# A decoder layer in full precision on one Trainium2 core: each weight split once, the pair of parts kept in DRAM

## The chip, the core and the metric

The kernel runs on one core of one Trainium2 chip. A core has five engines that run side by side and wait for one another by semaphores: TensorE (PE in the profile; its weight loads are PEld), VectorE (DVE), ScalarE (ACT), GpSimd (POOL) and SyncE (SP), which here issues nearly all transfers. SBUF is the on-chip memory with 128 partitions, PSUM the small one that TensorE writes, DRAM the large one outside. The metric is the device time of one execution in microseconds, as the median of several runs.

## What is computed

One inference step of a one-layer decoder on 2048 prompt tokens and 32 sampled tokens (8 sequences of 4), model width 1024. An mLSTM group and a sliding-window attention group share one input projection and one output projection; a squared-ReLU MLP of width 4096 and a gated embedding follow.

```python
def decoder_layer(x, p, lp, state):
    xn = rms_norm(x, lp['norm_mix_pre'])
    qk_raw, v_m, o_m, gates, q_a, k_a, v_a = split_projection(xn @ lp['w_in'])
    ...
    mix = jnp.concatenate([y_m, y_a], axis=-1) @ lp['w_out']
    x = x + rms_norm(mix, lp['norm_mix_post'])
    u = rms_norm(x, lp['norm_ffn_pre'])
    f = jnp.square(jax.nn.relu(u @ lp['w_up'])) @ lp['w_down']
    x = x + rms_norm(f, lp['norm_ffn_post'])
    x = x + jax.nn.sigmoid(x @ lp['w_pgate']) * (p @ lp['w_pproj'])
```

All of it is in float32. The weights are w_in (1024 x 2312), w_out (1024 x 1024), w_up (1024 x 4096), w_down (4096 x 1024), w_pgate (1024 x 1024) and w_pproj (256 x 1024).

## The kernel before

**Products in two parts.** A float32 matrix is split into a high part, rounded to the type that TensorE takes in one pass (fp32r), and a low part, the remainder. A product of two matrices is then three products of parts: high by high, high by low, low by high (`mm3`). The split of a weight is `wsplit`: ScalarE casts the tile into `wh` (L246), and VectorE or GpSimd subtracts, `wl = w - wh` (L247); `weng` gives every second one to VectorE (`LODVE = 2`).

**Stages.** The tokens go in chunks of 128-token blocks, `CHUNKS` = four of three blocks and two of two. First `project` runs for each of the six chunks: gates and window keys (gv), window queries (qa), mLSTM queries and keys (qk), values (v) and output gates (o). The windowed attention and the mLSTM of a chunk run beside the projection as side streams. Then three `GROUPS` of two chunks each go through the output projection (`mix_mm`, tile mo), the MLP in 16 steps of 256 hidden columns (tiles up and dn), and the gated embedding (`gate_mm`, tiles pv and pg). In an MLP step from `FAST` = 4, 2, 2 on (one number for each group), the first product is done for both chunks together in seven products of half blocks, Winograd's form of Strassen's; its weights are blocks of w_up or sums of blocks, made from two tiles `wb` by additions on VectorE and GpSimd (`product`). The sampled tokens go with the last chunk of the projection and with the last group; their attention (`decode`) runs beside the first MLP steps of group 0.

**Weights.** `plan()` lists every weight in the order in which it is taken, 948 in all, and `Ring.take(n)` makes the next n. Each is a tile of 128 x 512 (528 for gates and keys). Making one means: a load of 256 KB into a raw tile `wr` (pool of 5; L308 rows, L317 the head rows of w_out in two halves, L325 blocks of two row tiles, L334 window queries in a changed order of columns), then the split into a high and a low tile (`wh`, `wl`, pool of 7 each). Step weights of `product` come from `wb` tiles of 512 KB (L264, pool of 4). Weights of w_in are taken once for each of the six chunks. Those of w_out, w_pgate and w_pproj are taken once for each chunk of each group, again six times; w_up and w_down once for each group (the rows of w_down of step 0 twice). Each time they are loaded and split anew.

**Order.** The matrix work is issued in the order of the program: `Flow` keeps it so, and estimates the passed time of TensorE (`tick`, `wait`, `drain`) to decide when a side stream may put in its next piece. The instructions of the other engines, and the transfers on SP, are put in an order by a planner that runs through the program ahead of time; on the chip each engine and SP then run in just that order. So a transfer whose data or whose slot is late holds up all transfers behind it.

A weight of a `take(4)` stays in its slot until the last product that reads it; with seven slots, three are then left for what follows.

## Time and profile before

| | |
|---|---|
| Median of three runs | 2709.64 us (2708.26 to 2717.78) |
| Span of the profiled execution, first to last instruction | 2703.7 us |
| Mean granted TensorE clock | 0.978 of full speed |
| Read from DRAM, written | 266.64 MB, 28.31 MB |
| Mean transfer rate | 110 GB/s |
| Packets under 2 KB | 139039 of 227600 |

The page states the span of the profiled execution; its time with what lies around the span is not listed apart from the three runs, whose median lies 5.9 us above the span. The slices of the page give the mean transfer rate and the busy share of the 16 transfer engines in 40 equal stretches of 67.6 us: the projection fills the first ten, group 0 runs to 1467 us, group 1 to about 2158 us. "DMA share" in a table of stretches is that busy share; a stretch can come out above 1 because a packet's time is counted where it starts. A row of a timeline gives start, duration, engine, line, operation, what it writes and reads, and in brackets how long the engine had been idle and what ended that. "PEclk" is the granted clock, 1.00 at full speed.

### The profile page before, as it was taken

To read this page: it belongs to the slowest core of one execution; us is meant where nothing else is said; L and a number is where in the kernel's file an instruction comes from. 1 tells how busy PE (TensorE), PEld (TensorE's weight loads), DVE (VectorE), ACT (ScalarE), POOL (GpSimd) and SP (SyncE) were. 2 spreads that over 40 slices of the span, in tenths; PEclk is the share of its full clock that TensorE was granted. 3 is DMA by queue.
4 is the path that set the end of the run, shared out by engine and by line. 5 is a ranking of instruction groups with operands and counts; after the bars stand their busy time and mean duration, and the time that the engine had idled before them with its cause. 6 is when DMAs were issued, how large, how long until landed. Compare 5 with 4: busy or idle time off the path is not lost. (4 is left out here: it accounts for less than half of the span.)

```text
span 2703.7 us, 40778 instructions
## 1 busy us (share of the span) xinstructions
PE 2562.9 (95%) x14282; PEld 2223.0 (82%) x14282; DVE 1818.0 (67%) x3443; ACT 1367.8 (51%) x2909; POOL 1125.9 (42%) x1033
## 2 busy tenths in 40 slices
PE   7999999998899999999999999999999999999998
PEld 7787878777677788899977889988887778999986
DVE  7686877777665485555576775666557468777775
ACT  5656566656454443444444654443345365444463
POOL 3233333233241134444443444444444354676652
PEclk9999999999899999999999999999999999999998
DMA  6433343344566221222156522222215554222234
GB/s 184 116 99 105 108 114 106 108 118 131 126 191 109 84 82 63 63 72 77 47 181 194 186 83 83 65 71 63 63 47 162 173 190 132 90 80 84 92 116 127
DMA packets 227600, 296.53 MB, mean 110 GB/s; under 512 B 29387, under 2 KB 139039, under 8 KB 227378
## 3 DMA queue, kind: packets, MB, share of 16 engines
q1 hardware_dynamic: 227346, 293.89, 36.7%
q8 instruction: 112, 1.84, 0.3%
q14 instruction: 94, 0.77, 0.1%
q10 hardware_dynamic: 48, 0.03, 0.0%
HBM read 266.64 MB, written 28.31 MB: 109 GB/s over the span
## 5 line engine op out<-in xcount | busy, mean ns | idle before, releaser
L247 POOL TENSOR_TENSOR wl<-wr,wh 128x512 fp32r<-128x512 f32 (+2 forms) x358 | 493.0, 1382 | 686.2 <-ACT wh L246 500.6
L246 ACT CAST wh<-wr 128x512 fp32r<-128x512 f32 (+2 forms) x716 | 412.0, 590 | 336.4 <-issue 83.3
L246 ACT CAST wh<-wb 128x512 fp32r<-128x512 f32 x280 | 170.8, 620 | 497.6 <-PE dn L143 256.6
L1631 DVE TENSOR_TENSOR f<-f,dn 128x512 f32<-128x512 f32 x420 | 283.7, 683 | 178.2 <-PE dn L143 176.8
L247 POOL TENSOR_TENSOR wl<-wb,wh 128x512 fp32r<-128x512 f32 x200 | 265.6, 1347 | 316.7 <-ACT wh L246 316.7
L247 DVE TENSOR_TENSOR wl<-wr,wh 128x512 fp32r<-128x512 f32 (+2 forms) x358 | 286.8, 805 | 160.9 <-ACT wh L246 151.3
L143 PE MATMUL dn<-wh,hh 128*128 128x512 f32 x896 | 358.7, 400 | 9.0 <-DVE f L1631 4.9
L143 PE MATMUL dn<-wh,hl 128*128 128x512 f32 x896 | 353.4, 394 | 1.5 <-DVE hl L226 1.5
L143 PE MATMUL dn<-wl,hh 128*128 128x512 f32 x896 | 353.5, 395 | 0.0
L1595 DVE TENSOR_TENSOR re<-up,re 128x384 f32<-128x384 f32 (+1 forms) x280 | 143.4, 512 | 213.4 <-PE up L143 212.5
L143 PEld LDWEIGHTS dn<-wh,hh 128*128 128x128 f32 x896 | 168.6, 188 | 57.2 <-DVE f L1631 13.2
L143 PEld LDWEIGHTS dn<-wh,hl 128*128 128x128 f32 x896 | 168.7, 188 | 42.1 <-DVE hl L226 3.0
L143 PEld LDWEIGHTS dn<-wl,hh 128*128 128x128 f32 x896 | 168.8, 188 | 35.0
L226 DVE TENSOR_TENSOR hl<-re,hh 128x384 fp32r<-128x384 f32 (+1 forms) x192 | 178.8, 931 | 27.4 <-ACT hh L225 26.2
L269 POOL TENSOR_TENSOR wb<-wb,wb 128x512 f32<-128x512 f32 x40 | 53.1, 1328 | 144.4 <-DMA wb<-in_w_up_dram 91.9
L1522 ACT ACTIVATE re<-re 128x384 f32<-128x384 f32 (+1 forms) x192 | 94.8, 494 | 5.8
L225 ACT CAST hh<-re 128x384 fp32r<-128x384 f32 (+1 forms) x192 | 92.5, 482 | 5.3
L950 DVE CUSTOM_DVE_ANT_0 s<-aS,cst,sink 128x256 f32<-128x256 f32 (+1 forms) x128 | 57.3, 470 | 50.9 <-PE aS L143 50.6
L1521 ACT ACTIVATE re<-re 128x384 f32<-128x384 f32 (+1 forms) x160 | 78.8, 493 | 16.1 <-DVE re L1595 11.1
L956 ACT ACTIVATE s<-s,swt 128x257 f32<-128x257 f32 (+1 forms) x128 | 63.2, 496 | 39.4 <-DVE swt L953 38.8
L247 DVE TENSOR_TENSOR wl<-wb,wh 128x512 fp32r<-128x512 f32 x80 | 70.6, 883 | 0.4 <-ACT wh L246 0.4
L277 POOL TENSOR_TENSOR wb<-wb,wb 128x512 f32<-128x512 f32 x40 | 52.3, 1307 | 40.8 <-DVE wl L247 40.7
(1660 smaller groups left out, 7267.9 us busy)
## 6 DMA issues: line engine op xcount, KB each, us to landing
wr<-in_w_down_dram SPq DMA_DIRECT2D x204, 256.0 KB
wr<-in_w_in_dram SPq DMA_DIRECT2D x168, 256.0 KB
wb<-in_w_up_dram SPq DMA_DIRECT2D x80, 512.0 KB
wr<-in_w_pgate_dram SPq DMA_DIRECT2D x96, 256.0 KB
wr<-in_w_in_dram SPq DMA_DIRECT2D x96, 128.0 KB
wr<-in_w_out_dram SPq DMA_DIRECT2D x48, 256.0 KB
wr<-in_w_out_dram SPq DMA_DIRECT2D x96, 128.0 KB
x<-in_x_prompt_dram SPq DMA_DIRECT2D x16, 512.0 KB
```

The source lines that it names most:

```text
L143: ins = self.pe.matmul(out, lhsT, rhs, start=start, stop=stop)
L225: act.copy(hi, src)
L226: dve.tensor_tensor(lo, src, hi.bitcast(F32), ALU.subtract)
L246: act.copy(hi, src)
L247: (eng or weng()).tensor_tensor(lo, src, hi.bitcast(F32), ALU.subtract)
L269: next(eng).tensor_tensor(a21, a21, a22, ALU.add)
L950: dve.tensor_tensor_reduce(s_[:, s, lo : 2 * P], pS[:, s, lo:], bias[:, j, lo:], 1.0 if s == 0 else 0.0625, sink[:, h : h + 1], ALU.add, A ...
L956: act.activation(e_, e_, AF.Exp, bias=nm[:, s : s + 1], accum_out=sm[:, s : s + 1])
L1521: act.activation(t, src, AF.Relu)
L1522: act.square(t, t)
L1595: add = lambda out, a, b: dve.tensor_tensor(out, a, b, ALU.add)
L1631: dve.tensor_tensor(out(i), out(i), ps[i], ALU.add)
```

## The change

The high and the low part of a weight are now one tile of 128 x 2 x 512 with a tag of its own, still seven of them (`RAWS, PAIRS = 5, 7`). Each entry of the plan has a key that names the weight. At the first use of a key the weight is loaded and split as before; if the plan uses the key again, the pair is also stored to a tile in DRAM (`keep`, 512 KB). At each later use one load brings the pair (`get`), with no raw tile, no cast and no subtraction. This holds for the sums of blocks in `product` too: their tiles `wb` and additions are there at the first use only. The window queries are brought into their changed order of columns by the load itself now, in four transfers of 256-byte pieces in place of two of 512-byte pieces and two splits of half tiles.

```diff
+        def tile(self, n):
+            self.n += 1
+            t = self.pair.tile([P, 2 * WT], F32R, tag="w", name=f"{self.nm}{self.n}")
+            return t[:, : 2 * n].rearrange("p (e n) -> p e n", e=2)
+
+        def keep(self, key, t):
+            self.kept[key] = dram.tile(list(t.shape), U32, name=f"{self.nm}k{len(self.kept)}")
+            dma(self.kept[key], t.bitcast(U32))
+
+        def get(self, key, n, make):
+            t = self.tile(n)
+            if key in self.kept:
+                dma(t.bitcast(U32), self.kept[key])
+            else:
+                make(t[:, 0], t[:, 1])
+                if self.uses[key] > 1:
+                    self.keep(key, t)
+            return t[:, 0], t[:, 1]
...
+        def product(self, key, i, src):
+            def make(h, l):
+                if i == 0:
+                    self.blocks = []
+                    for e in range(2):
+                        t = self.wide.tile([P, KT // 2, 2 * P], F32, tag="w", name=f"{self.nm}b{self.n}{e}")
+                        dma(t, src[e * 512 : (e + 1) * 512].rearrange("(k p) n -> p k n", p=P))
+                        self.blocks += [t[:, :, :P], t[:, :, P:]]
...
+                wsplit(h, l, (a11, a12, a11, a22, None, a21, a12)[i], next(eng))
...
+            if i == 4 and key not in self.kept:
+                t = self.last
+                if self.uses[key] > 1:
+                    self.keep(key, t)
+                v = t[:, 0], t[:, 1]
+            else:
+                v = self.get(key, 512, make)
+            return [t.rearrange("p (k n) -> p k n", k=4) for t in v]
+
+        def set_plan(self, plan):
+            plan = list(plan)
+            for key, _ in plan:
+                self.uses[key] = self.uses.get(key, 0) + 1
+            self.plan = iter(plan)
...
-        def row(self, src, n):
-            r, h, l = self.tiles()
-            dma(r[:, :n], src)
-            wsplit(h[:, :n], l[:, :n], r[:, :n])
-            return h, l
+        def row(self, key, src, n):
+            def make(h, l):
+                raw = self.load(n)
+                dma(raw, src)
+                wsplit(h, l, raw)
+
+            return self.get(key, n, make)
...
+        def pairs(self, key, segs):
+            def make(h, l):
+                raw = self.load(512)
+                v = raw.rearrange("p (k j s c) -> p k j s c", k=2, j=2, s=2)
+                for s, src in enumerate(segs):
+                    for k in range(2):
+                        dma(v[:, k, :, s], src[:, k].rearrange("p (j c) -> p j c", j=2))
+                wsplit(h, l, raw)
+
+            return [v.rearrange("p (k n) -> p k n", k=2) for v in self.get(key, 512, make)]
```

`plan()` yields a key with each entry, such as ("v", k, off) for rows of w_in, (name, k, half) for rows of w_out, w_down, w_pgate and w_pproj, ("p", s, i) for the products of a step. Nothing else of the kernel changes: the stages, the order of the matrix work and the other pools stay.

More of the change, by code (lines that the diff above doesn't have):

```diff
@@ L280, in block @@
-        def block(self, src, eng):
-            self.n += 1
-            v = []
-            for t in "hl":
-                t = self.pair.tile([P, WT], F32R, tag=t, name=f"{self.nm}{t}{self.n}")
-                v.append(t[:, :512].rearrange("p (k n) -> p k n", k=4))
-            wsplit(*v, src, eng)
-            return v
+            self.plan, self.ready, self.kept, self.uses = None, [], {}, {}
+        def tile(self, n):
+            self.n += 1
+            t = self.pair.tile([P, 2 * WT], F32R, tag="w", name=f"{self.nm}{self.n}")
+            return t[:, : 2 * n].rearrange("p (e n) -> p e n", e=2)
@@ new lines, in load @@
+        def load(self, n):
+            return self.raw.tile([P, WT], F32, tag="r", name=f"{self.nm}r{self.n}")[:, :n]
+        def product(self, key, i, src):
[6 more added lines that the diff above has]
+                        self.blocks += [t[:, :, :P], t[:, :, P:]]
+                a11, a21, a12, a22 = self.blocks
+                eng = iter([dve if e == "d" else pool for e in UENG[i]])
+                h, l = [v.rearrange("p (k n) -> p k n", k=4) for v in (h, l)]
+                if i == 2:
+                    next(eng).tensor_tensor(a21, a21, a22, ALU.add)
+                    next(eng).tensor_tensor(a11, a21, a11, ALU.subtract)
+                elif i == 3:
+                    self.last = self.tile(512)
+                    wsplit(*[self.last[:, e].rearrange("p (k n) -> p k n", k=4) for e in range(2)], a22, next(eng))
+                    next(eng).tensor_tensor(a22, a22, a11, ALU.subtract)
+                elif i == 6:
+                    next(eng).tensor_tensor(a12, a12, a11, ALU.subtract)
+                wsplit(h, l, (a11, a12, a11, a22, None, a21, a12)[i], next(eng))
[7 more added lines that the diff above has]
+            return [t.rearrange("p (k n) -> p k n", k=4) for t in v]
@@ new lines, in heads, with multi, make @@
+        def heads(self, key, src, j, n):
+            def make(h, l):
+                raw = self.load(n)
+                for s in range(2):
+                    o = s * 256 + j * AD
+                    dma(raw[s * AD : (s + 1) * AD], src[o : o + AD])
+                wsplit(h, l, raw)
+            return self.get(key, n, make)
+        def multi(self, key, srcs, kn, n):
+            three = lambda v: v.rearrange("p (k n) -> p k n", k=kn)
+            def make(h, l):
+                raw = self.load(kn * n)
+                for off, w, s in srcs:
+                    dma(three(raw)[:, :, off : off + w], s)
+                wsplit(h, l, raw)
+            return [three(v) for v in self.get(key, kn * n, make)]
@@ L390, in plan @@
                             for e in range(2):
-                                yield lambda: ring.row(w_pp[e * P : (e + 1) * P, hs], 512)
-                        yield lambda: ring.row(w_pg[k * P : (k + 1) * P, hs], 512)
-    ring.plan = plan()
+                                yield row(w_pp, e, half)
+                        yield row(w_pg, k, half)
+    ring.set_plan(plan())
     tpA = ctx.enter_context(tc.tile_pool(name="tpA", bufs=1))
```

103 lines of the change are left out of this document (33 added, 70 removed).

## The prediction

> **What bounds the kernel now.** I read the page from the top: the span, the busy shares, the 40 slices, then the groups. PE is the bound, and the engines that do the splitting are not.
>
> ```profile
> span 2703.7 us, 40778 instructions
> PE 2562.9 (95%) x14282; PEld 2223.0 (82%) x14282; DVE 1818.0 (67%) x3443; ACT 1367.8 (51%) x2909; POOL 1125.9 (42%) x1033
> ...
> PE   7999999998899999999999999999999999999998
> ...
> q1 hardware_dynamic: 227346, 293.89, 36.7%
> ...
> L247 POOL TENSOR_TENSOR wl<-wr,wh 128x512 fp32r<-128x512 f32 (+2 forms) x358 | 493.0, 1382 | 686.2 <-ACT wh L246 500.6
> L246 ACT CAST wh<-wr 128x512 fp32r<-128x512 f32 (+2 forms) x716 | 412.0, 590 | 336.4 <-issue 83.3
> L246 ACT CAST wh<-wb 128x512 fp32r<-128x512 f32 x280 | 170.8, 620 | 497.6 <-PE dn L143 256.6
> ...
> wr<-in_w_pgate_dram SPq DMA_DIRECT2D x96, 256.0 KB
> ```
>
> PE is idle for 2703.7 - 2562.9 = 141 us, and no more than that, with the clock lost after the idle stretches, can come back. A table by stretch says where it is not:
>
> ```profile
> core 0: us, PE busy (x) PEld busy (x) DVE busy (x) ACT busy (x) POOL busy (x), PEclk, DMA share, GB/s
> 972.00:1366.00 394.00, 393.98 (x1956) 353.02 (x1955) 235.24 (x352) 170.40 (x319) 187.07 (x140) 1.00 0.23 73
> 2285.00:2600.00 315.00, 310.04 (x2120) 288.36 (x2120) 237.03 (x364) 160.27 (x332) 219.39 (x204) 1.00 0.28 88
> ```
>
> These are the Strassen steps of groups 0 and 2 (group 1 lies between, nines in the slices). PE is full; split work removed there returns nothing. What is left are single waits in the projection and at the seams between stages. PE's timeline shows those in which a weight split takes part:
>
> ```profile
> 181.43 0.88 PE L147 MATMUL aT<-ident,s 128*128 128x128 f32 x3 [3.76 <-DVE s L960]
> 306.07 0.68 PE L147 MATMUL aT<-ident,s 128*128 128x128 f32 x4 [3.86 <-DVE s L960]
> 429.99 0.87 PE L147 MATMUL aT<-ident,s 128*128 128x128 f32 x3 [3.85 <-DVE s L960]
> 556.32 1.09 PE L147 MATMUL aT<-ident,s 128*128 128x128 f32 x4 [2.44 <-ACT wh L246]
> 642.83 0.58 PE L143 MATMUL qk<-x5h,wh 128*128 128x256 f32 x1 [4.97 <-ACT wh L246]
> 2211.34 0.80 PE L143 MATMUL mo<-wl,yt21h 128*128 128x512 f32 x1 [2.16 <-DVE wl L247]
> 2637.37 0.50 PE L143 MATMUL pg<-wl,xt20h 128*128 128x512 f32 x1 [1.85 <-DVE wl L247]
> ```
>
> Each wait is followed by a stretch at a reduced clock:
>
> ```profile
> 305.00:310.00 5.00, 3.93 (x17) 3.90 (x18) 4.60 (x9) 2.96 (x7) 2.09 (x3) 0.67 0.41 108
> 555.00:560.00 5.00, 3.69 (x14) 3.33 (x15) 5.00 (x10) 3.94 (x10) 3.60 (x3) 0.66 0.10 15
> 640.00:645.00 5.00, 1.61 (x6) 1.32 (x7) 3.59 (x11) 3.93 (x11) 2.15 (x2) 0.62 0.13 18
> ```
>
> **The change in counts.** The plan has 948 weights, 250 of them different; 242 come back, in 698 later uses. Before there are 716 + 280 = 996 splits (48 of the plan's weights are split in two pieces); after there are 250. So 746 casts leave ACT, at (412.0 + 170.8)/996 = 0.585 us, 436 us of its 1368, and as many subtractions leave POOL and DVE. Bytes: a weight is 256 KB raw, a pair 512 KB. First uses still load 55 MB and now also store 242 pairs, 127 MB; later uses load 366 MB in pairs where the same uses loaded about 163 MB raw. The queue goes from 294 MB to about 625.
>
> **What is gained.** In chunks 1 to 3 the wait of aT is for the softmax chain on VectorE, which stands in a queue that is busy without a break; splits stand in that queue:
>
> ```profile
> L247 DVE TENSOR_TENSOR wl<-wr,wh 128x512 fp32r<-128x512 f32 (+1 forms) x4 | 2.4, 602 | 0.0
> ```
>
> This is the stretch from 287 to 306 us, ahead of the wait at 306. Without these four the wait falls from 3.86 to about 1.5 us, and the slow clock (0.33 x 5 = 1.65 us) should go: 4.05 each, **12.2 us** for three. What is late next is the softmax itself. The waits of chunks 4 and 5 end on a cast of a weight: 2.44 + 1.7 (0.34 x 5) and 4.97 + 1.5 (estimated: of the 0.38 x 5 = 1.9 part lies in the wait), **10.6 us**; what comes next is the pair's landing, which needs only a free slot. On clock, the Trainium skill ("TensorE: Matmul & The Clock Gate", section "What's actually happening") has the clock fall after an idle window of about 3.4 us; the row at 555 us has it at 0.66 behind a wait of only 2.44. By the page that 1.7 us would have another cause and stay; the sum would be 1.7 us smaller. I go by the row.
>
> The waits on wl itself are 2.16 and 1.85 above and three more:
>
> ```profile
> PE qa L143 <- DVE wl L247: 2.5, 3, 0.8
> ```
>
> 6.5 us in all; a late load can take the place of a late split, so I count half, **3.3 us**. Bounds of the whole gain: 0 and 29. Taken: 26. The splits taken from the full Strassen steps count nothing: PE hides them.
>
> **What is paid.** All transfers go through one queue, so the question is how fast it moves pairs. The mean of the queue is 293.89 MB/(0.367 x 2703.7 us) = 296 GB/s of full share; the best stretch, with 4 KB rows of x in it, gives 383/1.04 = 368. A pair is 4 KB a partition, nearest to the second, but its stores have no near row: I take the middle, 332, and keep both ends.
>
> ```profile
> 30.00:35.00 5.00, 5.00 (x33) 4.79 (x32) 2.75 (x5) 3.46 (x8) 1.22 (x2) 1.00 1.04 383
> ...
> 5.00:45.00 40.00, 34.73 (x212) 32.48 (x212) 26.42 (x49) 25.64 (x57) 16.55 (x21) 1.00 0.74 219
> ...
> 716.00:762.00 46.00, 39.97 (x159) 29.82 (x160) 27.08 (x39) 21.13 (x40) 16.39 (x13) 0.92 0.77 183
> 811.00:879.00 68.00, 63.52 (x346) 53.78 (x345) 34.30 (x86) 32.86 (x69) 13.06 (x10) 0.92 0.68 109
> ...
> 1383.00:1425.00 42.00, 41.72 (x197) 33.95 (x196) 25.42 (x43) 19.36 (x36) 14.25 (x12) 1.00 0.66 205
> 1425.00:1467.00 42.00, 42.00 (x189) 34.19 (x188) 23.53 (x33) 17.94 (x31) 13.82 (x10) 1.00 0.63 193
> ...
> 2190.00:2222.00 32.00, 29.55 (x138) 23.38 (x137) 26.27 (x49) 21.33 (x46) 19.40 (x12) 0.95 0.67 222
> ```
>
> - *Chunk 0* (5 to 45 us): 0.74 x 40 = 29.6 us of transfers now. Added are 12 stores, 6.3 MB (19 us; 17 to 21), and the q weights of the windows in 256-byte pieces for 512 (0 to 7 us, I take 3.5). 52 us into 40: 12 over. Stores at the end of the stretch hold up nobody until a slot is wanted: **8 us**, bounds 0 and 18.
> - *First mix and first MLP step* (716 to 762): 35.4 us now, and some nine stores left after the seven that fit ahead, 4.7 MB, 14 us: 4 over. 811 to 879: 46 us and 5.3 MB more, 16 us, 62 of 68: fits. **4 us**, bounds 0 and 8.
> - *First gate chunk* (1383 to 1425): 27.7 us and 13 stores, 6.8 MB, 20.5 us: 48 of 42. **6 us**, bounds 0 and 9.
> - *Later mix and gate chunks*: 1425 to 1467 has 26.5 us and 5.2 MB more, 16 us: 42.3 of 42. 2190 to 2222 has 21.4 and 4.2 MB more, 12.7: 34 of 32. **3 us**, bounds 0 and 10.
> - *Strassen steps*: group 0 stores 69.2 MB in 394 us, 208 us at 332 beside 91 of now; group 2 loads 51 MB more, 155 beside 88 in 315. Both fit, **0**; if that cover went, at 296 GB/s, they would still fit (234 + 91, 173 + 88).
> - *Fewer weights ahead*: now five raw tiles and seven pairs run ahead of PE, later seven pairs alone, and the four of a take are held to its end. SP is in order, and a store whose data is late holds all loads behind it:
>
> ```profile
> SPq L989 <- ACT ya L988: 46.3, 12, 6.2
> ```
>
> A load issued up to 6.2 us late was covered by raw tiles; with three free slots it may reach PE. **5 us**, bounds 0 and 15 (a third of 46.3). Each new store also waits on SP for its split, with loads behind it; those are priced in the first three items. A later load waits for its store to have landed, but the nearest pair of the two, the step 0 rows of w_down, is a stage apart.
> - *Issue time on SP*, by the median of the row below: in chunk 0 the window weights take 32 issues for 16, 16 x 0.43 = 7 us of SP's time, spread over some 25 us; later chunks and the head rows of w_out take one issue for two. **0**, and a loss of at most 7 in chunk 0, inside that item's bounds.
>
> ```profile
> L334 SPq DMA_DIRECT2D wr<-in_w_in_dram x96: 367/429/1809, 13.7 to 603.0; - x96
> ```
>
> Paid: 8 + 4 + 6 + 3 + 5 = 26 us. The sum of 26 gained and 26 paid is 0. The page gives a span of 2703.7 us for the execution it shows; the median, 2709.6, lies 5.9 above, and I put the sum there: **2710 us**.
>
> The Trainium skill ("DMA: Bandwidth & Descriptors", section "Bandwidth") gives about 358 GB/s as what memory allows one core when its neighbour streams too, and more when alone. At 358 the first four items would come to some 15 us, an estimate from that figure, and the total 6 us lower. The 383 in the row above is more than the figure, so the trace does not show it as a limit here.
>
> **Rivals.** *The transfers stay hidden* (faster). For it: the queue's share is 36.7% now and by the middle rate about 70% after; the Strassen steps have room. Against: the stretches above with two thirds of the queue taken already. Only the lookahead's 5 us would be paid against 26 to 29 gained: 2686 to 2689. *The queue becomes the bound where pairs are made or taken fastest* (slower). One mechanism: a pair costs two raw loads later, three at its first use, and chunk 0, the first gate chunk and the two-block mix have no room. At the mean rate of 296 the items are 18 + 5 + 9 + 10 + 5 = 47, so 2731; with the gains half lost as well, since a wait for a landing costs clock like any other, 2744. It decides from a rate below about 315 GB/s for pairs. Against it: large rows have run faster than that. *The later uses do not all load* (the change does not do what it says): a key that never matches would leave 996 splits and only add stores. The keys in the diff are tuples of the same constants in each pass, so I give it no chance of weight.
>
> **Chances.** No change that can be told, 0.40; hidden transfers, 0.28; the queue as bound, 0.32. A measurement of this kernel tells a difference of about 0.5%, 13.5 us, from none. The likeliest case alone is 2696 to 2723. The range takes in the gain at its bound with nothing paid (2709.6 - 29 = 2681) and the paid side at 296 with half the gains and a little more: 2681 to 2758.
>
> **What would show it.** Right: ACT's casts of weights 250 instead of 996; q1 near 625 MB; the aT waits of chunks 1 to 3 under 2 us; no wait on wh at qk in chunk 5; PE still full from 972 to 1366. Wrong: waits of PE that end on a DMA into the pair tile, above all in the Strassen steps; PE idle in chunk 0 by more than 20 us; a queue rate in the first gate chunk far from 332 GB/s; aT waits unchanged, which would say that the softmax chain and not the splits was late.

## The result, and the profile after

The changed kernel takes **2700.73 us** (median of six runs, 2693.66 to 2707.11), the kernel before in the same comparison 2712.85 (six runs, 2707.39 to 2720.20). The ratio is **0.9946**, with a 95% interval of 0.9929 to 0.9964: 0.54% faster. The execution that was profiled took 2707.11 us, the longest of the six, with a span of 2705.3 us; the other spans are 2691.8 to 2700.0. So the profiled execution shows none of the median's gain, and stages are compared below with that in mind.

From the page of the changed kernel: the span and busy times, the transfer queue, the two groups of casts, and the counts of pair loads and stores.

```profile
span 2705.3 us, 38958 instructions
...
PE 2562.3 (95%) x14282; PEld 2227.0 (82%) x14282; DVE 1439.4 (53%) x3109; ACT 980.7 (36%) x2163; POOL 410.6 (15%) x517
...
q1 hardware_dynamic: 233490, 624.44, 68.0%
...
L248 ACT CAST w<-wr 128x512 fp32r<-128x512 f32 (+1 forms) x152 | 93.4, 619 | 132.0 <-DMA wr<-in_w_up_dram 29.5
...
L248 ACT CAST w<-wb 128x512 fp32r<-128x512 f32 x98 | 60.4, 621 | 199.7 <-PE dn L145 134.4
...
w<-wk SPq DMA_DIRECT2D x678, 512.0 KB
wk<-w SPq DMA_DIRECT2D x238, 512.0 KB
```

The change does what it says: 152 + 98 = 250 casts of weights, 624 MB through the queue. VectorE, ScalarE and GpSimd lose 379, 387 and 715 us of work, and TensorE's busy and idle time stay where they were. The queue moves 624.44 MB/(0.68 x 2705.3 us) = 339 GB/s of its full share, where 332 was assumed. The time has moved between stages. The table gives the length of each stage, from the first matmul of one to the first matmul of the next on TensorE's timeline; the last column is a control (the run e9_none_kept below: the new ring with nothing kept, and the window weights brought by two transfers as before).

| stage (us) | before | after | after - before | control |
|---|---|---|---|---|
| up to chunk 1's gates | 131.2 | 154.7 | +23.5 | 130.1 |
| chunk 1 | 124.2 | 116.3 | -7.9 | 128.8 |
| chunk 2 to chunk 5's output gates | 421.0 | 393.2 | -27.8 | 430.4 |
| from there to group 0's MLP (with the output projection) | 130.1 | 133.6 | +3.5 | 125.7 |
| group 0's MLP | 576.2 | 600.5 | +24.3 | 572.0 |
| group 0's gate | 84.3 | 93.1 | +8.8 | 84.6 |
| group 1's output projection | 73.7 | 70.5 | -3.2 | 73.8 |
| group 1's MLP | 531.9 | 520.2 | -11.7 | 533.3 |
| group 1's gate | 87.0 | 86.8 | -0.2 | 87.1 |
| group 2 up to its gate | 458.2 | 452.6 | -5.6 | 457.3 |
| group 2's gate to the end of the span | 85.9 | 83.8 | -2.1 | 84.3 |

The stages in which chunk 0 and group 0 make the pairs lose (+23.5 + 3.5 + 24.3 + 8.8 = 60 us), the others return 58.5. How far can such a stage be trusted? Two profiles of one kernel (e1 and e16 below) agree within 0.9 us in every stage but two: 3.1 us up to chunk 1's gates, and 3.1 in group 0's MLP. A second profile of nearly the same kernel is that of e4 below, which adds work only from step 4 of group 2's MLP on: its span is 2690.1 us, 13.6 under before's, as the median would have it. It has +20.3 us up to chunk 1's gates, -3.2 from chunk 5's output gates to group 0's MLP, +23.2 in that MLP and +7.7 in the gate, with the other stages within 1.7 us of the column "after". So the signs of the large terms are the same; only the stretch to group 0's MLP, 6.7 us apart, changes its sign.

The sign that the prediction named for the chunks is there: over chunks 1 to 4 the softmax waits of aT are gone. From the tables of TensorE's waits, 170 to 600 us (us in total, times, longest), in before and in after:

```profile
PE aT L147 <- DVE s L960: 15.2, 9, 3.9
...
PE aT L149 <- DVE s L1012: 1.4, 3, 0.5
```

In their place stand few and larger waits, on TensorE's timeline (start, duration, instruction, idle time ahead of it and what ended it):

```profile
60.97 0.69 PE L145 MATMUL qa<-x0h,w 128*128 128x384 f32 x1 [4.87 <-ACT w L248]
...
619.22 0.58 PE L145 MATMUL qa<-x5h,w 128*128 128x256 f32 x1 [4.45 <-DMA w<-wk]
...
888.43 0.69 PE L145 MATMUL up<-ut00h,w 128*128 128x384 f32 x1 [20.85 <-ACT w L248]
...
1449.77 1.22 PE L145 MATMUL pg<-w,xt01h 128*128 128x512 f32 x2 [4.05 <-DMA w<-wk]
...
2242.94 1.19 PE L145 MATMUL dn<-w,hh 128*128 128x512 f32 x2 [4.81 <-DMA w<-wk]
```

Two of the five are at a first use (they end on a cast; ScalarE stood 21.7 us for the raw load ahead of the second one), three wait for a pair. The 20.85 us lie within MLP step 1 of group 0; the expectations below put it "before step 1".

By stretch, the changed kernel's Strassen steps in groups 0 and 2 (the columns are those of the tables in the prediction):

```profile
972.00:1366.00 394.00, 392.65 (x1963) 353.88 (x1962) 231.29 (x346) 165.60 (x305) 178.01 (x134) 1.00 0.68 247
2300.80:2593.30 292.50, 292.50 (x2030) 278.77 (x2029) 142.47 (x299) 71.79 (x169) 9.11 (x52) 1.00 0.72 257
```

and the kernel before over its steps 2 to 13 of group 2:

```profile
2285.10:2565.70 280.60, 275.64 (x1875) 255.21 (x1874) 212.28 (x324) 139.28 (x289) 195.48 (x180) 1.00 0.29 91
```

Those twelve steps last 280.6/12 = 23.4 us before; the thirteen of after 292.5/13 = 22.5, with TensorE busy for all of it. The prediction had read 310 of 315 us as "full"; the last 2% were a wait. That is half of the 0.9 us a step (0.41 idle, 4.96 us over twelve steps); the other half is TensorE's busy time for as many matmuls, 22.97 us a step before and 22.50 after with the clock at 1.00 in both, and why it falls is not known.

### The profile page after: what moved, and what is told of

Its sections match the earlier page's. It is cut to its first block, busy times and chain, and to the rows that moved or that the text cites. A ratio compares the mean times of both kernels' runs of the same rounds, so it can differ in the third digit from the quotient of the medians.

```text
span 2705.3 us, 38958 instructions
## 1 busy us (share of the span) xinstructions
PE 2562.3 (95%) x14282; PEld 2227.0 (82%) x14282; DVE 1439.4 (53%) x3109; ACT 980.7 (36%) x2163; POOL 410.6 (15%) x517
## 3 DMA queue, kind: packets, MB, share of 16 engines
q1 hardware_dynamic: 233490, 624.44, 68.0%
## 4 chain that ended last, share of the span: by engine, by line
PE 78%; DMA 8%; DVE 8%; ACT 2%; POOL 2%; issue 2%; SPq 1%; POOLq 0%; ACTq 0%; DVEq 0%
PE up L145 23%; PE dn L145 21%; PE mo L145 5%; PE pg L145 5%; PE v L145 3%; PE o L145 3%; DMA w<-wk 2%; PE gv L145 2%; PE qa L145 2%; PE pv L145 1%; PE aT L149 1%; PE aO L145 1%; PE qk L145 1%; DMA out_dram<-scs 1%; PE aS L145 1%
## 5 line engine op out<-in xcount | busy, mean ns | idle before, releaser
L145 PE MATMUL dn<-w,hh 128*128 128x512 f32 x1792 | 567.8, 398 | 15.4 <-DMA w<-wk 9.6
L145 PEld LDWEIGHTS dn<-w,hh 128*128 128x128 f32 x1792 | 334.3, 189 | 95.1 <-issue 11.3
L145 PE MATMUL dn<-w,hl 128*128 128x512 f32 x896 | 354.3, 395 | 0.0
L145 PEld LDWEIGHTS dn<-w,hl 128*128 128x128 f32 x896 | 169.3, 189 | 39.4
L249 POOL TENSOR_TENSOR w<-wr,w 128x512 fp32r<-128x512 f32 (+1 forms) x76 | 105.4, 1389 | 303.2 <-ACT w L248 199.7
L248 ACT CAST w<-wr 128x512 fp32r<-128x512 f32 (+1 forms) x152 | 93.4, 619 | 132.0 <-DMA wr<-in_w_up_dram 29.5
L248 ACT CAST w<-wb 128x512 fp32r<-128x512 f32 x98 | 60.4, 621 | 199.7 <-PE dn L145 134.4
L145 PE MATMUL up<-ut00h,w 128*128 128x384 f32 x320 | 88.7, 348 | 24.7 <-ACT w L248 23.5
L249 POOL TENSOR_TENSOR w<-wb,w 128x512 fp32r<-128x512 f32 x70 | 93.8, 1359 | 54.1 <-ACT w L248 54.1
L145 PE MATMUL up<-ut01h,w 128*128 128x384 f32 x320 | 88.9, 340 | 0.0
L145 PEld LDWEIGHTS up<-ut00h,w 128*128 128x128 f32 x320 | 60.2, 194 | 27.1 <-ACT w L248 24.3
```

Source lines behind the costliest of these rows:

```text
L145: ins = self.pe.matmul(out, lhsT, rhs, start=start, stop=stop)
L248: act.copy(hi, src)
L249: (eng or weng()).tensor_tensor(lo, src, hi.bitcast(F32), ALU.subtract)
```

## The experiments

All runs start from the changed kernel (line numbers of its quotes are those of each run's own file), and each was read by stage as above. "c1" is the first matmul of chunk 1's gates, "MLP 0" the length of group 0's MLP.

**Is the new ring itself worth anything?** The ring lost its separate high and low tiles as well. In e9_none_kept nothing is kept (and a window weight takes two transfers again):

```diff
-                self.uses[key] = self.uses.get(key, 0) + 1
+                self.uses[key] = self.uses.get(key, 0) + (0)
```

> The new ring with nothing kept: every weight is loaded and split at each use as in before, with the window weights by two transfers, 5 raw tiles, and 7 pairs in which high and low part share a tile. If the ring itself costs nothing, it is before: 2700 to 2716 us, chunk 1's gates at 129 to 134 us, Strassen steps of group 2 of 23 to 24 us. If the gain of after came from the new ring and not from keeping, it is 2680 to 2695.

2709.26 us, beside 2710.76 for the kernel before (one run, against the median of seven). c1 is 130.1, group 2 lasts 457.3 us up to its gate. The ring by itself moves up to 14 us between stages (chunks 1 to 5 lose 14, the stretch to group 0's MLP and that MLP get 9 back) and nothing in the time that one run could tell. So gain and loss of the change come from keeping, and from the four small transfers of a window weight, which this run does not have.

**Chunk 0.** Two theories: the stores stand in SyncE's queue ahead of raw loads, or the window weights' four small transfers cost. e1_window_two undoes the second:

```diff
-                v = raw.rearrange("p (k j s c) -> p k j s c", k=2, j=2, s=2)
                 for s, src in enumerate(segs):
-                    for k in range(2):
-                        dma(v[:, k, :, s], src[:, k].rearrange("p (j c) -> p j c", j=2))
-                wsplit(h, l, raw)
+                    dma(v[:, :, s * 128 : s * 128 + 128], src)
...
+                for s in range(2):
+                    wsplit(hv[:, :, :, s], lv[:, :, :, s], rv[:, :, s])
```

> The window weights are loaded by two transfers each (512-byte pieces) and split in two halves, as in the kernel before; all pairs are still stored at their first use. The measure is the first matmul of chunk 1's gates: 131.2 us in the profile of before, 154.7 us in that of after (23.5 late). Theory S, the stores stand in SyncE's queue waiting for their split, and the next raw loads behind them: it stays at 148 to 155. Rival W, the four small transfers of each window weight are the loss: it falls to 131 to 140. The span then falls by the same amount.

e2_projection_late keeps the projection's pairs at their second use:

```diff
                 make(t[:, 0], t[:, 1])
-                if self.uses[key] > 1:
+                self.uses[key] -= 1
+                if self.uses[key] in range(1, self.left(key)):
                     self.keep(key, t)
...
+        def left(self, key):
+            return len(CHUNKS) - 1 if key[0] in "gaqv" else 99
```

> The projection's pairs are stored in chunk 1 instead of chunk 0; chunk 1 splits its weights again, chunks 2 to 5 load pairs; the window weights keep their four small transfers. Theory S: chunk 1's gates start at 131 to 143, and the loss moves to chunk 1, where 5 to 20 us appear between its gates and chunk 2's (124.2 us apart in before, 116.3 in after). Rival W: chunk 1's gates still start at 148 to 155.

e3_late_and_two has both edits.

> Both edits: stores in chunk 1, and two transfers for each window weight. Both theories together leave nothing in chunk 0: chunk 1's gates start at 131 to 136. If they start later than 140, something else in chunk 0 costs, the shared ring of pairs (7 pairs, where the kernel before had 5 raw tiles and 7 pairs) above all.

| | c1 (us) | chunk 1 (us) | time of one run (us) |
|---|---|---|---|
| after | 154.7 | 116.3 | 2707.11 |
| e1, two transfers | 142.7 (the same kernel in e16: 145.8) | 115.6 | 2677.26 |
| e2, stores in chunk 1 | 133.5 | 126.6 | 2677.97 |
| e3, both | 128.3 | 125.0 | 2676.09 |

The kernel before stood at 2705.15 us beside these. e1's c1 falls between the two ranges of its expectation, so neither theory holds alone: the small transfers account for 9 to 12 of the 23.5 us (for 5 without stores), the stores for 21 when the small transfers stay and for 14 to 17.5 when they are gone. The parts add up to more than the whole, as they would where both meet in one queue. Stored in chunk 1, the same pairs cost less: chunk 1 then lasts as long as in before (125.0 and 126.6 against 124.2), and against loading pairs there, splitting once more and storing costs 9 to 11 us. The store itself shows no cost there: the control splits in chunk 1 without storing and takes 128.8.

SyncE's timeline of the changed kernel shows what happens (start, time, instruction, number in a row):

```profile
21.87 5.04 SPq L372 DMA_DIRECT2D wr<-in_w_in_dram  x10
33.38 0.34 SPq L268 DMA_DIRECT2D wk<-w  x1
33.77 0.47 SPq L372 DMA_DIRECT2D wr<-in_w_in_dram  x1
34.34 0.75 SPq L268 DMA_DIRECT2D wk<-w  x1
35.13 3.92 SPq L372 DMA_DIRECT2D wr<-in_w_in_dram  x7
```

Ten raw transfers are issued by 26.9 us; then comes a store, whose split is not done, and SyncE issues nothing for 6.5 us. SyncE's waits from 5 to 45 us put a name to it:

```profile
SPq L268 <- POOL w L249: 11.5, 4, 6.4
```

The stretch in between, in after:

```profile
27.00:33.00 6.00, 5.55 (x36) 4.80 (x36) 2.31 (x6) 2.49 (x5) 0.94 (x1) 0.86 0.15 29
```

and in before:

```profile
27.00:33.00 6.00, 6.00 (x38) 5.79 (x37) 3.41 (x6) 1.76 (x5) 1.15 (x3) 1.00 1.04 334
```

The transfer engines, full at 334 GB/s before, stand at a share of 0.15 for those six microseconds. That is not bandwidth, but order. Two runs asked whether order is all. e5_stores_gpsimd (with two transfers for a window weight) takes the stores out of SyncE's queue:

```diff
-            dma(self.kept[key], t.bitcast(U32))
+            nc.gpsimd.dma_start(self.kept[key], t.bitcast(U32))
```

> Window weights by two transfers as in the run e1_window_two, and the 242 stores of pairs issued from GpSimd's queue instead of SyncE's, with the same bytes at the same places. In e1_window_two chunk 1's gates start 11.5 us later than before, with the stores moved to chunk 1 2.9 us earlier. Theory S, the stores stand in SyncE's queue waiting for their split and hold up the raw loads behind them: without them in that queue chunk 1's gates start at 126 to 134 us. Rival B, the stores cost by their bytes or by holding the pairs' buffers: it stays at 139 to 145.

c1 is 143.2 us: rival B's figure, and no better than e1. The time is 2696.5 us beside 2709.04 for before, since group 0's MLP got longer too (609.4: step 0 lasts 76.7 us for e1's 66.1, and most Strassen steps 32.2 to 32.5 for 31.4). e12_quarter_stores keeps the waits and takes the bytes away:

```diff
+                elif key[0] in "gaqv" and self.uses[key] == len(CHUNKS) - 1:
+                    d = dram.tile([P, 2, n // 4], U32, name=f"{self.nm}q{self.n}")
+                    dma(d, t[:, :, : n // 4].bitcast(U32))
```

> As e3_late_and_two, and in chunk 0 a quarter of each pair is stored, to tensors that nothing reads: 36 more stores at the places of e1_window_two's, waiting for the same splits, of 128 KB instead of 512. Chunk 1's gates start at 128.3 us without stores and at 142.7 with whole ones. Theory B, the bytes of the stores cost: 128 to 133 us. Theory S, the stores' waits in SyncE's queue cost, whatever they move: 138 to 144. In between, both: 133 to 138.

c1 is 139.2 us: 10.9 over the run without stores, of the 14.4 to 17.5 that whole ones cost, so a quarter of the bytes leaves three fifths to three quarters of the loss. That is theory S's figure. Each run refutes the other's rival as long as one asks for a single cause. The stretch from 8 to 42 us tells more. In e3_late_and_two, without stores:

```profile
8.00:42.00 34.00, 32.11 (x192) 29.91 (x193) 22.16 (x40) 23.26 (x51) 14.35 (x18) 1.00 0.73 224
```

in e1_window_two, with stores in SyncE's queue:

```profile
8.00:42.00 34.00, 27.66 (x151) 24.85 (x152) 15.08 (x26) 15.00 (x33) 8.77 (x13) 0.85 0.73 233
```

in e12_quarter_stores:

```profile
8.00:42.00 34.00, 28.48 (x161) 25.83 (x162) 15.65 (x29) 17.31 (x38) 10.69 (x15) 0.90 0.65 179
```

and in e5_stores_gpsimd, where no store stands in SyncE's order:

```profile
8.00:42.00 34.00, 27.97 (x171) 25.29 (x171) 18.52 (x26) 15.04 (x33) 16.35 (x25) 1.00 1.03 361
```

TensorE does 32.1 us of work in 34 without stores, and about 28 in each of the three others, but the transfer share (the last but one column) tells them apart: 0.65 and 0.73, a queue with room that is fed too late, against 1.03 at 361 GB/s, a queue that is full. By these rows order is the first limit, and the bytes are the next one right behind it: taking the stores out of SyncE's queue returned nothing, and three quarters of their bytes a quarter to two fifths of the loss. How SyncE is held in e12 is seen on its timeline, where loads go out by ones and twos between the stores, and in its waits at those stores (5 to 45 us):

```profile
25.89 0.53 SPq L282 DMA_DIRECT2D wq<-w  x1
26.46 0.61 SPq L378 DMA_DIRECT2D wr<-in_w_in_dram  x1
27.75 0.52 SPq L282 DMA_DIRECT2D wq<-w  x1
28.32 1.16 SPq L378 DMA_DIRECT2D wr<-in_w_in_dram  x2
...
SPq L282 <- DVE w L249: 6.0, 4, 2.7
```

What is late in e5 is the softmax chain of a side stream, TensorE's longest wait up to 150 us; VectorE stood 5.4 us of it waiting for a load that went out at 61.8 us and had landed by 69.9. GpSimd, which now issues the stores, waits at them too (its waits from 5 to 110 us):

```profile
PE aT L149 <- DVE s L1014: 10.5, 1, 10.5
...
POOL wk L268 <- DVE w L249: 9.0, 5, 5.5
```

So e5 moves the stores' waits into another engine's order and does not take them away. That its loss comes from the full queue alone is not shown.

The Trainium skill ("DMA: Bandwidth & Descriptors", section "Issuing engines are not separate DMA queues") says that another issuing engine saves only the issuing engine's own time; the share of 1.03 in e5's stretch agrees, the same transfer engines are full.

**Group 0's output projection and first MLP steps.** After, e4, e1 and e16 have 600.5, 599.4, 591.9 and 595.0 us for MLP 0, so the loss is 16 to 24 us. e6_mix_late (with two transfers for a window weight) stores the weights of the output projection and of steps 0 and 1 in group 1, by e2's rule with other counts:

```diff
+            if key[0] == "u" or "w_down" in key[0] and 2 <= key[1] < 4:
+                return 2
+            return 4 if ("w_out" in key[0] or key[0] == "heads") or "w_down" in key[0] and key[1] < 2 else 99
```

> Window weights by two transfers, and the weights of the output projection and of MLP steps 0 and 1 are stored in group 1 instead of group 0, so that group 0 splits them at each use as the kernel before and neither stores nor loads a pair there. From group 0's first output projection to its gates pass 666.1 us in before, 696.0 in after, 683.6 in e1_window_two, with one idle time of 18 to 21 us of TensorE before step 1. Theory R, the pair loads and stores push step 1's raw loads behind the decode states' 16 stores in SyncE's queue: 666 to 672 us, no idle time over 8 us there, and group 1 up to 10 us longer. Rival D, the decode states' stores alone make it, wherever the pairs are: 680 to 690 us.

MLP 0 takes 572.4 us, the control's 572.0 (from the first output projection to the gate, as the expectation counts, 649.2, lower still than theory R's 666 to 672): with no pair made or loaded in the output projection and in steps 0 and 1, group 0's MLP loses nothing. But group 1's output projection then lasts 99.5 us, where it takes 70.6 with pairs loaded and 73.7 with everything split as before; theory R allowed 10 us for all of group 1. In all 2692.21 us beside 2709.04: the loss was moved, not removed. That stretch in e6:

```profile
1445.30:1544.80 99.50, 80.48 (x326) 61.58 (x325) 42.63 (x70) 35.76 (x70) 21.83 (x18) 0.91 0.80 284
```

and the same stage in before:

```profile
1467.00:1540.70 73.70, 71.36 (x325) 57.48 (x325) 50.55 (x77) 42.63 (x84) 33.05 (x25) 1.00 0.60 190
```

e7_states_scalar moves the decode states' 16 stores to ScalarE's queue:

```diff
-                dma(c_out[e, h], cs[er, :, h, 0:128])
-                dma(n_out[e, h], cs[er, :, h, 128])
+                nc.scalar.dma_start(c_out[e, h], cs[er, :, h, 0:128])
+                nc.scalar.dma_start(n_out[e, h], cs[er, :, h, 128])
```

> Window weights by two transfers, and the 16 stores of the decode states issued from ScalarE's queue instead of SyncE's; pairs are kept as in after. Theory R: step 1's raw loads have nothing to wait behind, the idle time of 18 to 21 us before step 1 falls under 8, and group 0 takes 664 to 674 us from output projection to gates. If the raw loads are late for want of raw tiles or pairs, it stays at 680 to 690.

The long idle time is gone (the longest there is 8.7 us), and MLP 0 is 591.6 us as in e1: the wait broke up into others with the same sum (steps 0 and 1 last 84.2 and 46.2 us for e1's 66.1 and 64.2). From output projection to gate it is 684.2 us, the figure of the expectation's other reading, raw loads that are late for want of raw tiles or pairs, and not theory R's. The order behind those stores set where the loss shows, not how large it is. 2680.64 us, beside 2709.04.

e8_three_raw_eight tries more lookahead:

```diff
-RAWS, PAIRS = 5, 7
+RAWS, PAIRS = 3, 8
```

> Window weights by two transfers, with 3 raw tiles and 8 pairs in place of 5 and 7 (the same memory). In the runs so far TensorE waits 2.8 to 5.6 us for a pair's load at six starts of a stage, some 22 us in all (near 601, 745, 1421, 2185, 2216 and 2221 us). If the pairs' number sets how early a load starts, one more pair takes a quarter to a half of it: 5 to 11 us from 600 us on, against up to 5 us lost in chunk 0 with fewer raw tiles. If those waits come from the order in SyncE's queue, nothing changes there.

The eighth pair returns little where pairs are loaded, and the waits of TensorE that end on a pair's landing are not fewer (20.8 us in all, 18.6 in e1): group 2 takes 446.4 us up to its gate, for 448.8 to 452.1 in e1, e2, e12 and e16, and the wait of 4 us at chunk 5's window weights only moves to the next weights. With three raw tiles chunk 0 loses 4 to 7 us more and MLP 0 takes 621.2, its Strassen steps 32.0 to 34.6 us for 31.4: 2707.91 us, beside 2709.04. First uses need raw tiles more than later ones need pairs.

**Group 2's steps.** The prediction had no term here, and 0.9 us a step came. Does GpSimd hold VectorE up? VectorE's groups in the kernel before, steps 2 to 13 (busy us, mean ns):

```profile
L226 DVE TENSOR_TENSOR hl<-re,hh 128x272 fp32r<-128x272 f32 x48 | 55.9, 1165 | 5.6 <-ACT hh L225 4.4
L1595 DVE TENSOR_TENSOR re<-up,re 128x272 f32<-128x272 f32 x84 | 36.3, 432 | 33.5 <-PE up L143 33.2
L247 DVE TENSOR_TENSOR wl<-wr,wh 128x512 fp32r<-128x512 f32 x24 | 30.9, 1287 | 0.5
L1631 DVE TENSOR_TENSOR f<-f,dn 128x512 f32<-128x512 f32 x48 | 30.5, 675 | 0.0
```

and after:

```profile
L1647 DVE TENSOR_TENSOR re<-up,re 128x272 f32<-128x272 f32 x91 | 40.0, 440 | 86.7 <-PE up L145 86.7
L1683 DVE TENSOR_TENSOR f<-f,dn 128x512 f32<-128x512 f32 x52 | 35.8, 688 | 30.5 <-PE dn L145 30.5
L228 DVE TENSOR_TENSOR hl<-re,hh 128x272 fp32r<-128x272 f32 x52 | 22.9, 440 | 0.4
```

The subtraction hl, with both inputs in SBUF, falls from 1165 to 440 ns; re and f, each with one input in PSUM, do not change. In before, all of TensorE's waiting in these steps was for f:

```profile
PE dn L143 <- DVE f L1631: 4.4, 11, 0.8
```

e4_extra_subtractions brings operations of that kind back, without use:

```diff
...
+            mode = ("p", "d", "dp")[(s - 4) // 3]
+            for e in engs:
+                if e in mode:
+                    o = self.load(512)
+                    eng = dve if e == "d" else pool
+                    eng.tensor_tensor(o, t[:, 0].bitcast(F32), t[:, 1].bitcast(F32), ALU.subtract)
```

> The kernel after, with extra subtractions in the Strassen steps of group 2, whose results nothing uses, read from the loaded pair: in steps 4 to 6 eleven on GpSimd a step, in steps 7 to 9 four on VectorE, in steps 10 to 12 both (what the kernel before ran there), in steps 13 to 15 none. Steps last 22.5 us in after and 23.2 to 23.9 in before; the subtraction for the hidden layer's low part (128x272, VectorE) takes 440 ns in after and 1121 in before. Theory P, GpSimd's subtractions hold up VectorE's: 900 to 1200 ns in steps 4 to 6 and 10 to 12, 440 in 7 to 9 and 13 to 15; steps of 22.5 to 23.2 us with GpSimd's alone, 22.5 with VectorE's alone, 23.2 to 23.9 with both. Rival Q, VectorE's own four subtractions are what made the steps longer: 23 or more in steps 7 to 9 and 22.5 in steps 4 to 6, with 440 ns throughout.

The three settings in that order, GpSimd's alone, VectorE's alone, both (VectorE's groups over 2332.3 to 2399.8, 2399.8 to 2467.3 and 2467.3 to 2534.8 us):

```profile
L228 DVE TENSOR_TENSOR hl<-re,hh 128x272 fp32r<-128x272 f32 x12 | 7.9, 656 | 0.1
...
L296 DVE TENSOR_TENSOR wr<-w 128x512 f32<-128x512 f32 x12 | 8.2, 686 | 1.0 <-DMA w<-wk 1.0
L228 DVE TENSOR_TENSOR hl<-re,hh 128x272 fp32r<-128x272 f32 x12 | 5.3, 439 | 0.1
...
L296 DVE TENSOR_TENSOR wr<-w 128x512 f32<-128x512 f32 x10 | 8.3, 835 | 0.8 <-DMA w<-wk 0.6
L228 DVE TENSOR_TENSOR hl<-re,hh 128x272 fp32r<-128x272 f32 x12 | 7.5, 621 | 0.9 <-ACT hh L227 0.9
```

The slowing is GpSimd's doing (656 and 621 ns with it, 439 without, on both of VectorE's kinds), though smaller than before's 1165; but every step lasted 22.5 us, so neither theory's figure for the steps came. e14_other_engines moves the real splits (base: only the projection kept, so that the MLP splits at each use):

```diff
-                eng = iter([dve if e == "d" else pool for e in UENG[i]])
+                eng = iter([dve if e == "d" or key[1] >= 9 else pool for e in UENG[i]])
...
-                wsplit(h, l, raw)
+                wsplit(h, l, raw, pool if "w_down" in key[0] and 2 * FS <= key[1] < 9 * FS else None)
```

> As e10_projection_only (the MLP's weights split at each use, group 2's steps 23.3 to 23.9 us), with other engines for the weights' subtractions and sums: in steps 2 to 8 the two of the down weights that VectorE had go to GpSimd, in steps 9 to 15 all of the products' go to VectorE, where GpSimd keeps two a step. Theory P, GpSimd's subtractions hold up VectorE's on the hidden layer, so that the sums into f come late: in group 2 steps 2 to 8 stay at 22.9 to 23.9, steps 9 to 15 fall to 22.5 to 22.9, with 440 to 650 ns for the hidden layer's subtraction, though VectorE has nine operations more. Theory Q, VectorE's own number of weight subtractions makes the steps longer: 22.5 to 22.8 in steps 2 to 8, over 23.8 in steps 9 to 15.

With more on GpSimd, the steps of group 2 took 24.5 to 27.2 us (steps 2 to 8); with nearly all on VectorE, 23.1 to 23.8 (steps 9 to 13); e10, which divides them as before, has 23.3 to 23.9. Neither theory's ranges came. VectorE's rows in steps 2 to 7:

```profile
L228 DVE TENSOR_TENSOR hl<-re,hh 128x272 fp32r<-128x272 f32 x24 | 19.6, 816 | 14.9 <-ACT hh L227 14.9
...
L249 DVE TENSOR_TENSOR w<-wb,w 128x512 fp32r<-128x512 f32 x12 | 12.0, 1001 | 1.3 <-ACT w L248 1.3
```

and from 2460 to 2575 us, in steps 9 and up:

```profile
L249 DVE TENSOR_TENSOR w<-wb,w 128x512 fp32r<-128x512 f32 x36 | 23.8, 684 | 0.2 <-ACT w L248 0.2
...
L228 DVE TENSOR_TENSOR hl<-re,hh 128x272 fp32r<-128x272 f32 x20 | 8.7, 433 | 0.0
```

So both ends lose: GpSimd stretches VectorE's operations from 684 to 1001 ns and from 433 to 816, and without it VectorE does each quicker but has more of them, and TensorE waits for it all the same. Shown is that these steps are longer when splits are in them, in each of the three divisions between the engines, than when pairs are loaded; and that GpSimd's subtractions slow VectorE's. What share of the 0.9 us is the one or the other stays open. 2705.3 us, beside 2706.69.

**What to keep.** e10_projection_only and e11_projection_strassen keep less (window weights by two transfers, the projection's pairs from chunk 1 on):

```diff
-                self.uses[key] = self.uses.get(key, 0) + 1
+                self.uses[key] = self.uses.get(key, 0) + (key[0] in "gaqv")
```

and for the second one

```diff
+                self.uses[key] = self.uses.get(key, 0) + ((key[0] in "gaqv" or key[0] == "p" or "w_down" in key[0] and key[1] >= 4))
```

> Only the projection's 36 pairs are kept (stored in chunk 1, loaded in chunks 2 to 5); everything behind it splits at each use as before; window weights by two transfers. In e3_late_and_two the projection stands 30.6 us ahead of before at chunk 5's output gates. Theory L, the loss behind it (18 to 30 us up to group 0's gate) comes from stores and loads of pairs there: group 0's gate keeps the lead (26 to 34 us ahead), steps of group 2 last 23 to 24 us again, and the time is 2670 to 2682. If the lead is lost in group 0 all the same, another resource ends there: 2690 to 2705.

> As the run before, and the weights of MLP steps 2 and up (the products, and the down weights) are kept at their first use; the output projection, MLP steps 0 and 1 and the gate split at each use as before. Theory L: a first use costs 768 KB of the queue instead of 256, which is late where a stage uses a weight every 2.2 us (the output projection, the window weights, the gates) and free in the Strassen steps, where 11 weights take 31.4 us; a pair that is loaded returns little in the output projection and the gate. So the lead of the projection (30 us) stays, group 2's steps add 8 to 12 us, and the time is 2650 to 2668 us, 0.977 to 0.985 of before. If keeping the pairs of the output projection and the gate returned something, it is 2670 or more, behind e1_window_two and e3_late_and_two.

e10: 2676.11 us in one run. MLP 0 takes 574.1 us, group 0's gate 84.5 (93.1 after), so the lead of the projection is not lost. e11: 2666.3 us (four runs), ratio 0.9832 (0.9816 to 0.9849): both as theory L had it. Group 2 then takes 447.7 us up to its gate, for 460.1 in e10.

e13_first_steps_kept adds the up weights of steps 0 and 1 and step 1's down weights; e15_best takes step 0's up weights out again (this is e15's line):

```diff
+                self.uses[key] = self.uses.get(key, 0) + ((key[0] in "gaqv" or key[0] == "p" or key[0] == "u" and key[1] == 1 or "w_down" in key[0] and key[1] >= 2))
```

> As e11_projection_strassen, and the up weights of MLP steps 0 and 1 and the down weights of step 1 are kept too, from their first use in group 0: 12 more stores there, but no pair is loaded within group 0. From the MLP's start to the gate group 0 takes 576.5 us in e11 and 595.1 in e3_late_and_two (all kept). If the stores make that loss: 585 to 597 us. If the pairs that step 0 loads again, or the output projection's pairs, make it: 574 to 582. In group 1 the steps up to 3 gain 10 to 14 us, in group 2 those up to 1 between 6 lost and 3 gained.

> As e13_first_steps_kept without the up weights of step 0: kept are the projection's pairs (from chunk 1), the up weights of step 1, the products, and the down weights from step 1 on. e13 lost 6.4 us in group 0 by twelve stores and 5 us at the start of group 2's step 0, and gained 8 between groups 1's step 0 and step 1. With eight stores it should lose 3 to 5 in group 0 and nothing in group 2's step 0: 2655 to 2664 us, 0.979 to 0.983 of before. If step 0's stores were not the cost, it stays at 2664 or more.

e13 took 2664.16 us (one run): MLP 0 582.9, so twelve stores cost 6.4 us of the 18.6 between e11 and e3, between the two theories; group 1's MLP gains 10.0 (538.2 to 528.2). e15 took **2647.29 us** (five runs, 2642.71 to 2648.70), ratio **0.9768** (0.9746 to 0.9790), better than forecast: MLP 0 is 574.5 us, the eight stores cost nothing, group 1's MLP keeps its 528.2, and group 2 takes 442.4. From its page:

```profile
q1 hardware_dynamic: 230290, 537.37, 60.1%
```

It keeps fewer pairs than the changed kernel and moves 87 MB less. e16_window_two_timed runs e1's kernel, the smallest edit alone, six times:

> The kernel of e1_window_two, timed. In its one look chunk 1's gates started 12 us earlier than in after and group 0 lost 12 us less up to its gate; the second has no cause in the edit that we can name, so that it may be chance. With the first alone it is 2683 to 2692 us, 0.990 to 0.993 of before; with both 2674 to 2682, 0.986 to 0.989.

2680.41 us (six runs), ratio 0.9894 (0.9872 to 0.9917); the interval reaches into both of the expected ones. Beside after's ratio the window weights' transfers come to about half a per cent, 14 us (the two ratios are from different comparisons), of which chunk 0 shows 9 to 12; MLP 0 is 4 to 9 us shorter in the same profiles, and why is not known.

## Why the prediction was wrong

Forecast was 2710 us, no difference that can be told, as a sum of 26 us gained and 26 paid. It came out 0.54% faster. The time lies within the range; the terms of the sum did not hold. Two steps failed. For the gain, split work outside a few named waits was put at nothing ("PE is full; split work removed there returns nothing"): in the profiles group 1's MLP returned 11.7 us and group 2's steps 12, which had no term, and chunks 1 to 5 returned 35.7 for 22.8. For the cost, making a pair was priced by its bytes, and the store's wait for its split, said to be priced, was in no term: chunk 0 cost 23.5 for 8, and the way from group 0's output projection through its MLP 27.8 for 4 (20 in e4's profile). In the profiled execution the two sides cancel; in e4's profile 13.6 us are left, near the median's 12.

- **Chunks 1 to 5** (22.8 us forecast, with part of 3.3): 35.7 us (7.9 + 27.8). The mechanism was right, the aT waits and the wait on a cast at chunk 5's qk went; the size of the terms was low. By stretch, chunk 2 to chunk 5's output gates in before

```profile
255.40:676.40 421.00, 384.91 (x2647) 331.30 (x2646) 324.91 (x889) 256.79 (x659) 137.18 (x182) 0.98 0.40 114
```

and in after

```profile
271.00:664.20 393.20, 377.66 (x2647) 326.12 (x2646) 246.15 (x803) 183.41 (x495) 34.99 (x99) 1.00 0.63 211
```

TensorE's idle time falls from 36.1 to 15.5 us, and its busy time for the same 2647 matmuls by 7.2, with the clock at 1.00 for 0.98. The sum had five long waits and half of the short ones on wl. From chunk 2 on the four long ones make 15.1 us of before's idle time and all the others 21; in after the others are down to 11. Against the control, which splits at each use with the same ring, keeping returned 50 us in chunks 1 to 5. The new wait at chunk 5's window weights (4.45 us) was named, as "what comes next is the pair's landing".
- **Strassen steps** ("PE is full; split work removed there returns nothing"): right in group 0 and from step 2 on in group 1 (31.4 us a step, before and after), wrong in group 2, where 23.4 became 22.5. 310 of 315 us busy was taken for full, but a repeated wait of 0.4 us for f hides in such a share, and the busy time of the same matmuls fell as well. Group 2 returns only 5.6 of these 12 us up to its gate, since its output projection and steps 0 and 1 take 6.5 us longer; TensorE waits 12.5 us for pairs there (the row at 2242.94 is one of these waits). Group 1's MLP returned 11.7 us, 7.1 of it in steps 0 and 1 and 4.7 from step 15 to the gate, for which the sum had no term either.
- **Chunk 0** (8 us, bounds 0 and 18): 23.5, beyond the bound. The step that failed is that the item was summed in bytes only, with "each new store also waits on SP for its split, with loads behind it; those are priced in the first three items". Nothing in the three items priced it; in after SyncE waits up to 6.4 us for one such split. A queue with a share of 0.65 to 0.73 was late all the same (e12, e1); and the small transfers, 3.5 us there and "0" in issue time, cost 9 to 12.
- **First mix and first MLP step** (4 us, bounds 0 and 8): 3.5 + 24.3. "811 to 879 ... fits" was the false line: steps 0 and 1 lose 23 us. Left unkept (e11, e15) the MLP term is 0.3 and -1.7 us against before, so the loss comes from making and loading pairs there. By which way is open: e13's twelve stores alone cost 6.4 us, the decode states' stores set only where the loss shows (e7), fewer raw tiles make it larger (e8), and taking the stores out of SyncE's queue did not help (e5).
- **First gate chunk and later mix and gate chunks** (6 + 3): +8.8 in group 0's gate, -3.2 and -0.2 in group 1. The sum is near, but the place is not the one forecast. The gate's first chunk, which makes and stores the pairs, takes 42.5 us for 41.4 before; its second, which loads them, 50.6 for 43.0. SyncE issues the last of the stores ahead of those loads at 1434 us, seven us before the second chunk starts:

```profile
1440.80:1491.40 50.60, 46.29 (x193) 36.66 (x194) 15.03 (x24) 6.65 (x11) 0.00 (x0) 0.93 0.87 302
```

- **Fewer weights ahead** (5 us, bounds 0 and 15): TensorE's table of waits has 27.8 us that end on the landing of a pair (9.6 in dn, 7.3 in mo, 4.9 in pg, 4.4 in qa, 1.6 in others), above the bound. Part of it stands in the stages of the items above. e15, which keeps no pair of the output projection, the gate and step 0, has 4.3 us of them left. An eighth pair (e8) left these waits at 20.8 us, where e1 has 18.6, so that the number of pairs is not shown to be the cause.
- **The rate**: 339 GB/s for an assumed 332. By the rate alone the rival of the queue as bound was rightly not taken; transfers were late in places by what stands in front of what.

Gains of 12 to 13 us were missing in three places, and two costs were short by 15 and 24 us; that they nearly cancelled is chance. The kernel did get faster, which the prediction gave 0.28, but not by the mechanism that it had for this case: the transfers did not stay hidden.

## What to carry to other kernels

Ask for each use of a kept result, and not in the mean, how fast its stage takes the results: here first uses (raw load, split, store) were free in Strassen steps of 31.4 us for 11 weights as long as there were five raw tiles, and stages that make pairs lost 9 us in a gate (84 us for 40 weights), 26 in group 1's output projection (74 us for 32; at most 4 in group 0's, which lies among other work) and 24 at the start; keep only what is stored where there is room, and leave the rest as it was. A store that waits for its data holds back every load behind it in the same queue (here up to 6.4 us for one), so look at what is behind it before counting its bytes. An engine that is 98% busy need not be full: look whether the missing 2% are one wait that recurs in every step.

## What the runs showed of the hardware

VectorE's subtraction of two operands in SBUF depends on what GpSimd does at that moment: 128x272 took 440 ns alone, 656 and 621 beside e4's subtractions, 816 beside e14's splits and 1165 beside before's; 128x512 took 684 to 686 alone, 835 beside e4's and 1001 to 1287 beside splits; with one operand in PSUM the same kind of operation did not change (432 and 440 ns; 675 and 688). The Trainium skill ("SBUF — State Buffer", section "Who interferes with whom") states this rule: a VectorE instruction with two SBUF inputs contends with a GpSimd instruction that reads SBUF, one with at most one SBUF input, outside the 2-port modes in which it also uses the port pair that it shares with GpSimd, does not. The rows agree with both halves. So taking splits off GpSimd was a gain for VectorE, which the prediction had in no term.

Moving the same 242 stores from SyncE's queue to GpSimd's lifted the transfer share from 0.73 to 1.03 between 8 and 42 us and returned nothing, and it lengthened group 0's MLP from 591.9 to 609.4 us.
